# A hybrid encoder on one core: the first two weight jobs of a layer done by halves of the tokens

## The chip, the cores and the metric

The kernel runs on one core of one Trainium2 chip. The metric is the device time of one execution in microseconds; where several runs are given, their median.

## What is computed

Two layers, each with one mixer of two parallel groups, 256 tokens, model width 2048, all in float32. Cut to what matters here:

```python
x = layer_norm(x, ln_emb_g, ln_emb_b)
for l in range(DEPTH):                       # DEPTH = 2
    proj = einsum('bsd,de->bse', x, w_in[l])  # 2048 -> 6144
    u, g_ssm, q, k, v, g_attn = split(proj)
    y = u * ssm_d + s5_scan(u, forward) + s5_scan(u, reverse)
    y = gelu(y);  y = y * sigmoid(y @ w_glu[l] + b_glu[l]);  y_ssm = y * silu(g_ssm)
    lam = exp(sum(lambda_q1 * lambda_k1)) - exp(sum(lambda_q2 * lambda_k2)) + lambda_init
    o = diff_attention(rotary(q), rotary(k), v, lam)
    y_attn = rms_norm(o, attn_norm_g[l]) * (1 - lambda_init) * silu(g_attn)
    x = layer_norm(ALPHA * x + concat(y_ssm, y_attn) @ w_out[l], ln_g[l], ln_b[l])
return x
```

## The kernel before

Every large product is made of three float32r products: both operands are split into a high part, rounded to float32r, and a low part, the rest, and `mm3` (lines 167 to 170) adds high by high (line 168), high by low of the activations (line 169) and low of the weights by high (line 170).

The weights come in **jobs** of 512 by 256 values (`jobs`, line 124; 272 of them). `load` (line 143) fetches a job on SP's queue into one of four `raw` buffers; `do_split` (line 155) makes `wh` on ScalarE (line 162) and `wl` on VectorE (line 164), two jobs ahead of their use, in three buffers; `sub_step` (line 841) then issues 24 products of 128x128 weights by 256 tokens (2 column blocks, 4 contraction tiles, 3 products). The first eight jobs of a layer are the first two column blocks of the input projection, taken alternately for each quarter of the contraction, into two PSUM tiles `acc2`; every later block takes its four jobs one after the other.

The activations stand with the contraction on the partitions. They get there by the **layer norm** `ln_finish` (line 214), a generator that the program advances by `next(ln)`: moments on VectorE and GpSimd, `centre` (line 229) and `norm` (line 235) on VectorE, transposes on TensorE (line 248), and the split into `xh` (ScalarE, line 252) and `xl` (VectorE, line 253). It works on two sets of 128 rows (tokens), i = 0 and 1. Rows 0 come first for the first contraction tiles (four tiles before layer 0, eight before layer 1), then rows 1, then the rest of both. In the kernel before, the first product of a layer waits until rows 1 are there as well, since each takes all 256 tokens. Before layer 0 the input is loaded and normalised; before layer 1 the norm follows the last two output blocks of layer 0 (lines 987 to 1012), which are themselves done for rows 0 first, then for rows 1.

**Side work** runs between the jobs: `side` (line 778), called once a job, advances generators (`Lane`) for the SSM's tables (`ssm_tables`, line 295), operand loads and transposes (`ssm_load`, line 403; lines 421 and 446), the SSM's input, scan and output, the attention heads, and the stores of x for the residual. A generator's second yielded number is how many jobs it stays away.

The order in which instructions stand in each engine's queue is made by a scheduler that simulates the program's time; `after(ins)` (line 115) ties what is issued under it behind an instruction. SP's queue, like the others, is in order. Small loads stand in SP's queue among the weights: lambda's four vectors and the norm's gain `gsc` (`lam_of`, lines 661 and 673, called at the beginning of a layer), the tables' eight (lines 302 to 305), `ssm_d` (line 435), `b_glu` (line 955). `newest[0]` holds the latest weight load.

Of the kernel before, what the change touches and what calls it, by code (L numbers as in the profile page):

```python
# [8 lines left out]
F32 = mybir.dt.float32  # L9
F32R = mybir.dt.float32r  # L10
AF = mybir.ActivationFunctionType
# [9 lines left out]
KT = 4  # L21
# [11 lines left out]
RAW_BUFS = 4  # L33
SPLIT_AHEAD = 2
BUDGET = 1.6
# [2 lines left out]
LOAD_HOP = 10  # L38
SCAN_COST = 1.0
HEAD_HOPS = (1,1,2,2,2,3)  # L40


@with_exitstack
def kernel(
# [34 lines left out]
    def T(shape, tag, bufs=1, dt=F32):  # L79
        return sb.tile(shape, dt, tag=tag, name=tag, bufs=bufs)  # L80
# [33 lines left out]
    @contextmanager  # L114
    def after(ins):

        if ins is None:
            yield
        else:
            with tc.issue_after(ins):  # L120
                yield
# [16 lines left out]
        for cb in range(8):  # L138
            jobs += [(l, "out", cb, 0), (l, "out", cb, 1)]
    raws, split = {}, {}  # L140
    newest = [None]

    def load(i):
        if i >= len(jobs):
# [10 lines left out]
    def do_split(i, wh=None, wl=None, behind=None):  # L155
        if i >= len(jobs):
            return
        raw = raws.pop(i)
        if wh is None:
            wh = T([128, KT, 256], "wh", SPLIT_AHEAD + 1, F32R)  # L160
            wl = T([128, KT, 256], "wl", SPLIT_AHEAD + 1, F32R)
        A.copy(wh, raw)  # L162
        with after(behind):
            V.tensor_tensor(wl, raw, wh.bitcast(F32), sub)  # L164
        split[i] = (wh, wl)

    def mm3(o, lh, ll, rh, rl, first, last):
# [46 lines left out]
    def ln_finish(r, gt, bt, st, dst, box, ahead):  # L214


        pool = [None]

        def moments(i):
            mv = T([128, 2], "mv", 2)  # L220
            V.bn_aggr(mv, st[:, i].rearrange("p c s -> p (c s)"))
            rstd = T([128, 1], "rstd", 2)
            GP.tensor_scalar(rstd, mv[:, 1:2], EPS, None, add)
            pool[0] = GP.tensor_tensor(rstd, rstd, mhalf[:, 0:1], ALU.pow).ins
            return mv, rstd

        def centre(i, k0, nk, mv):
            cs = slice(k0 * 128, (k0 + nk) * 128)
            V.scalar_tensor_tensor(r[:, i, cs], r[:, i, cs], mv[:, 0:1], gt[:, cs], sub, mult)

        def norm(i, k0, nk, mv, rstd):
            cs = slice(k0 * 128, (k0 + nk) * 128)
            if dst is None or i == 0:
                centre(i, k0, nk, mv)
            last = V.scalar_tensor_tensor(r[:, i, cs], r[:, i, cs], rstd, bt[:, cs], mult, add)  # L235
            if dst is None:
                stores.append((xres[128 * i:128 * i + 128, cs], r[:, i, cs]))
            else:
                for j in range(2):
                    SY.dma_start(dst[2 * i + j][:, cs], r[64 * j:64 * j + 64, i, cs])  # L240
            return last.ins

        def trans(k0, nk, i0, ni):

            t = ss_bank([128, nk, 128 * ni])
            for k in range(nk):
                for i in range(ni):
                    PE.transpose(t[:, k, 128 * i:128 * i + 128],
                                 r[:, i0 + i, (k0 + k) * 128:(k0 + k + 1) * 128], ident)
            sl = (slice(None), slice(k0 % 8, k0 % 8 + nk), slice(128 * i0, 128 * (i0 + ni)))  # L250
            h, lo_ = box[0].h[k0 // 8][sl], box[0].l[k0 // 8][sl]
            A.copy(h, t)  # L252
            V.tensor_tensor(lo_, t, h.bitcast(F32), sub)  # L253

        mv, rstd = moments(0)
        if dst is None:
            box[0] = Pair()
        m0 = mv, rstd
        last = None
        for k0 in range(0, ahead, 4):  # L260
            nk = min(ahead - k0, 4)
            with after(last if k0 else None):
                last = norm(0, k0, nk, *m0)
            if dst is None:
                trans(k0, nk, 0, 1)
        yield
        mv, rstd = moments(1)
        if dst is None:
            box[0].more()
        if dst is not None:  # L270
            k0 = k1 = 0
            for nk in LAST_PIECES + (0,):
                if nk:
                    with after(last):
                        centre(1, k0, nk, mv)
                if k0:
                    last = norm(1, k1, k0 - k1, mv, rstd)
                k0, k1 = k0 + nk, k0
            return
        for k0, nk in ((0, 2), (2, 2), (4, 4), (8, 4), (12, 4)):  # L280
            for i, m in ((0, m0), (1, (mv, rstd)))[k0 < ahead:]:
                with after(last):
                    last = norm(i, k0, nk, *m)
            box[1] = last, pool[0]
            if dst is None:
                if k0 < ahead:
                    trans(k0, nk, 1, 1)
                else:
                    for k in range(k0, k0 + nk, 2):
                        trans(k, 2, 0, 2)  # L290
            if k0 != 0 or ahead < 8:
                yield


    def ssm_tables():
# [3 lines left out]
        ls = T([128, 2], "p_ls")  # L299
        for l in range(2):  # L300
            ps = slice(64 * l, 64 * l + 64)
            SY.dma_start(lr[ps].rearrange("g (d p) -> g d p", d=2), ssm_lam_re[l].rearrange("d g p -> g d p"))
            SY.dma_start(li[ps].rearrange("g (d p) -> g d p", d=2), ssm_lam_im[l].rearrange("d g p -> g d p"))
            for d in range(2):
                SY.dma_start(ls[ps, d:d + 1], ssm_log_step[l, d].unsqueeze(1))
        step = T([128, 2], "p_st")
        A.activation(step, ls, AF.Exp)
        for d in range(2):
            dsl = slice(64 * d, 64 * d + 64)
            V.tensor_scalar(zr[:, dsl], lr[:, dsl], step[:, d:d + 1], None, mult)  # L310
            V.tensor_scalar(zi[:, dsl], li[:, dsl], step[:, d:d + 1], None, mult)
        mag = t1
        A.activation(mag, zr, AF.Exp)
        yield 1.0, 1
# [88 lines left out]
    def ssm_load(l):  # L403
# [28 lines left out]
        z.dd = T([128, 16], "dd")  # L432
        GP.memset(z.dd, 0.0)
        for gi in range(4):
            SY.dma_start(
                z.dd[32 * gi:32 * gi + 16, :],
                ssm_d[l].rearrange("(q g c) -> g c q", g=4, c=16)[gi],
            )
        z.C = T([128, 2, 64, 16], "c8")
        Cv = z.C.rearrange("p r (o g) c -> p r o (g c)", o=8)  # L440
        yield 0.0, 1
# [213 lines left out]

    swap = list(range(8, 16)) + list(range(0, 8)) + list(range(16, 32))

    def lam_of(l):
        t = T([128, 4, 64], "on")
        for i, src in enumerate((lambda_q1, lambda_k1, lambda_q2, lambda_k2)):  # L660
            SY.dma_start(t[:, i, :], src[l:l + 1, :].to_broadcast([128, 64]))
# [10 lines left out]
        gs = T([128, 1], "gsc", 2)  # L672
        SY.dma_start(gs, attn_norm_g[l].unsqueeze(1))
        V.tensor_scalar(gs, gs, 1.0 - init, None, mult)
        return neg, gs

# [139 lines left out]
    box = {}  # L816
    ln = ln_finish(r, gt, bt, st, None, box, 4)
    for i in range(2):
        for c in range(8):
# [1 line left out]
        if i == 0:  # L821
            next(ln)
    for i in range(SPLIT_AHEAD):
        next(ln)
        do_split(i, behind=box[1][0])
        load(RAW_BUFS + i)
    ji = 0

# [9 lines left out]
    def acc_bank():  # L838
        return PS([128, 2, 256], "acc", 2)
# [19 lines left out]
    def block(hi, lo, n=4, tok_major=False):  # L859
        acc = acc_bank()  # L860
        for s in range(n):
            sub_step(acc, s, hi, lo, 0, n * KT - 1, tok_major)
        return acc

    for l in range(DEPTH):
        if l:
            next(ln)
        X = box[0]
        if l == 0:
            l_load = Lane(ssm_load(0), 1)  # L870
            l_tab = Lane(ssm_tables(), 1)
# [11 lines left out]
            z.ublocks = b + 1  # L883

        l_store = Lane(store_x(), 1.5)
        neg, gsc = lam_of(l)
        hi, lo = X.hi, X.lo
        acc2 = [acc_bank(), acc_bank()]
        for s in range(4):
            for b in range(2):  # L890
                sub_step(acc2[b], s, hi, lo, 0, 15, k_outer=True)
                if s == 3:
                    u_done(b, acc2[b])
                if b == 0 and s < 3:
                    next(ln)
            if s == 2:
                l_in = Lane(ssm_in(l), 3, after=[l_load, l_tab])
        l_in.after.append(l_store)
        for b in (2, 3):
            u_done(b, block(hi, lo))  # L900
        l_scan = Lane(ssm_scan(l), 5, after=[l_in])
        oT = T([128, 8, 256], "a8", 3)
        store = {}
# [48 lines left out]
        finish(l_out)  # L952
        V.tensor_tensor(z.yT, sgs, z.yT, mult)
        bg = T([128, 8], "bg", 2)
        SY.dma_start(bg, b_glu[l].rearrange("(o p) -> p o", p=128))
# [121 lines left out]
```

## Time and profile before

| | us |
|---|---|
| median of 3 runs | 1005.09 (1001.4 to 1006.62) |
| profiled execution, its own time | 1002.55 |
| span of that execution | 1000.8 |
| TensorE: products in flight | 955.8 |
| TensorE: weight loads | 926.8 |
| VectorE busy | 780.3 |
| ScalarE busy | 576.0 |

The profile shows one execution. PE is TensorE's products, PEld its weight loads, which overlap the products; DVE is VectorE, ACT ScalarE, POOL GpSimd, SP the queue that issues the DMAs here. A product's listed duration (about 0.28 us) is longer than the step from one product to the next, since products are pipelined; steps are read from the starts. A group of rows gives the line, the engine, the operation, the tile that it writes and the tiles that it reads; line numbers are those of the kernel before.

### The profile page before, as it was taken

The page shows a single profiled execution, that of the slowest core. Times are in us where ns is not written, and L with a number is a line of the kernel's source. Part 1 is how long each engine was busy: PE and PEld are TensorE (multiplying, and loading weights), DVE is VectorE, ACT ScalarE, POOL GpSimd, SP SyncE. Part 2 cuts the span into 40 slices and gives each one's busy share as a digit, 9 for nine tenths or more (in the row PEclk, how much of TensorE's full clock was granted, in tenths as well). Part 3 has the DMA queues.
Part 4 walks back from the last instruction along what each step waited for, and adds up shares of the span by engine and source line. Part 5 has one row for each costly group of instructions (what it writes and reads, how often), then busy time and mean ns, then how long its engine had stood idle before and what let it go on. Part 6 is the DMA issues. An engine that isn't in the chain of part 4 may idle for free.

```text
span 1000.8 us, 24625 instructions
## 1 busy us (share of the span) xinstructions
PE 955.8 (96%) x10304; PEld 926.8 (93%) x10304; DVE 780.3 (78%) x1353; ACT 576.0 (58%) x950; POOL 71.7 (7%) x103
## 2 busy tenths in 40 slices
PE   2999999999999998999979999999999999999995
PEld 2989988999999998999979989999999999999995
DVE  6875799899887786656588699899899759565676
ACT  2546588565575697545344585555556769843640
POOL 1000130210200000000011030010100100000001
PEclk9999999999999999999989999999999999999998
DMA  9898521545554643779875724555445454576953
GB/s 272 254 256 230 184 81 44 168 149 169 156 183 153 193 145 104 234 228 260 215 231 167 233 68 126 170 169 161 157 150 187 151 168 136 178 237 209 270 173 85
DMA packets 193167, 177.76 MB, mean 178 GB/s; under 512 B 37536, under 2 KB 185760, under 8 KB 193056
## 3 DMA queue, kind: packets, MB, share of 16 engines
q1 hardware_dynamic: 193056, 176.18, 58.7%
q8 instruction: 81, 1.33, 0.6%
q14 instruction: 30, 0.25, 0.1%
HBM read 165.02 MB, written 11.14 MB: 176 GB/s over the span
## 4 chain that ended last, share of the span: by engine, by line
PE 81%; DMA 7%; DVE 6%; ACT 3%; issue 1%; SPq 1%; POOL 0%; POOLq 0%; DVEq 0%; ACTq 0%
PE acc L168 23%; PE acc L169 23%; PE acc L170 23%; DMA raw<-in_w_out_dram 3%; PE ss L596 2%; DVE wl L164 2%; PE ss L501 1%; PE sc L707 1%; PE ss L735 1%; PE tp L473 1%; ACT wh L162 1%; PE tp L577 1%; DVE w L456 1%; DVE H L235 1%; DMA H<-in_x_dram 1%
## 5 line engine op out<-in xcount | busy, mean ns | idle before, releaser
L164 DVE TENSOR_TENSOR wl<-raw,wh 128x1024 fp32r<-128x1024 f32 x266 | 324.9, 1223 | 143.0 <-ACT wh L162 141.8
L162 ACT CAST wh<-raw 128x1024 fp32r<-128x1024 f32 x266 | 278.2, 1050 | 251.0 <-PE acc L169 118.7
L168 PE MATMUL acc<-xh,wh 128*128 128x256 f32 x1280 | 370.9, 290 | 0.8 <-ACT xh L252 0.5
L169 PE MATMUL acc<-xl,wh 128*128 128x256 f32 x1280 | 365.2, 286 | 0.8 <-DVE xl L253 0.7
L170 PE MATMUL acc<-xh,wl 128*128 128x256 f32 x1280 | 364.1, 285 | 1.1 <-DVE wl L164 1.1
L168 PEld LDWEIGHTS acc<-xh,wh 128*128 128x128 f32 x1280 | 245.5, 192 | 6.2 <-ACT xh L252 1.4
L169 PEld LDWEIGHTS acc<-xl,wh 128*128 128x128 f32 x1280 | 245.7, 192 | 2.4 <-DVE xl L253 1.5
L170 PEld LDWEIGHTS acc<-xh,wl 128*128 128x128 f32 x1280 | 245.6, 192 | 2.1 <-DVE wl L164 1.5
L168 PE MATMUL acc<-wh,xh 128*128 128x256 f32 x512 | 146.3, 286 | 0.0
L169 PE MATMUL acc<-wl,xh 128*128 128x256 f32 x512 | 145.4, 284 | 0.0
L170 PE MATMUL acc<-wh,xl 128*128 128x256 f32 x512 | 145.0, 283 | 0.0
L169 PEld LDWEIGHTS acc<-wl,xh 128*128 128x128 f32 x512 | 98.2, 192 | 0.2
L168 PEld LDWEIGHTS acc<-wh,xh 128*128 128x128 f32 x512 | 98.1, 192 | 0.1
L170 PEld LDWEIGHTS acc<-wh,xl 128*128 128x128 f32 x512 | 98.2, 192 | 0.0
L169 PE MATMUL acc<-wl,a 128*128 128x256 f32 x208 | 59.1, 286 | 2.1 <-DVE wl L164 2.1
L168 PE MATMUL acc<-wh,a 128*128 128x256 f32 x208 | 58.7, 284 | 0.0
L170 PE MATMUL acc<-wh,a 128*128 128x256 f32 x208 | 58.5, 283 | 0.0
L551 DVE TENSOR_TENSOR sa<-tab,H 128x256 f32<-128x256 f32 x126 | 53.0, 421 | 2.9 <-ACT H L504 0.7
L458 DVE TENSOR_TENSOR w<-w,x 128x512 f32<-128x512 f32 x64 | 45.6, 712 | 0.8
L169 PEld LDWEIGHTS acc<-wl,a 128*128 128x128 f32 x208 | 39.7, 191 | 3.3 <-DVE wl L164 3.3
L717 ACT ACTIVATE e<-sc,mx 128x256 f32<-128x256 f32 x64 | 29.5, 477 | 21.0 <-DVE mx L711 21.0
L168 PEld LDWEIGHTS acc<-wh,a 128*128 128x128 f32 x208 | 39.7, 191 | 0.4 <-ACT wh L162 0.4
(198 smaller groups left out, 1482.9 us busy)
## 6 DMA issues: line engine op xcount, KB each, us to landing
raw<-in_w_in_dram SPq DMA_DIRECT2D x192, 512.0 KB, 3.8
raw<-in_w_out_dram SPq DMA_DIRECT2D x64, 512.0 KB, 4.6
raw<-in_w_glu_dram SPq DMA_DIRECT2D x16, 512.0 KB, 4.4
xr<-xres SPq DMA_DIRECT2D x16, 256.0 KB, 4.3
xres<-H SPq DMA_DIRECT2D x14, 256.0 KB, 3.4
H<-in_x_dram SPq DMA_DIRECT2D x8, 256.0 KB, 5.9
u_dr<-ub SPq DMA_DIRECT2D x8, 256.0 KB, 3.3
a<-u_dr SPq DMA_DIRECT2D x8, 256.0 KB, 3.8
```

What stands on the lines that cost most here:

```text
L162: A.copy(wh, raw)
L164: V.tensor_tensor(wl, raw, wh.bitcast(F32), sub)
L168: PE.matmul(o, lhsT=lh, rhs=rh, start=first, stop=False, skip_group_check=True)
L169: PE.matmul(o, lhsT=lh, rhs=rl, start=False, stop=False, skip_group_check=True)
L170: PE.matmul(o, lhsT=ll, rhs=rh, start=False, stop=last, skip_group_check=True)
L235: last = V.scalar_tensor_tensor(r[:, i, cs], r[:, i, cs], rstd, bt[:, cs], mult, add)
L456: V.tensor_tensor(dst, t.unsqueeze(2).to_broadcast([128, 8, 16, 4]), M[:, m, gs, :].unsqueeze(3).to_broadcast([128, 8, 16, 4]), mult)
L458: V.tensor_tensor(w[:, r], w[:, r], x2, op)
L473: PE.transpose(t[:, pr, :], ws[o][:, ri, 2 * pr:2 * pr + 2].rearrange("p g c j -> p (g c j)"), ident)
L551: V.tensor_tensor(a.rearrange("p v q r g -> p v q (r g)"), lam, h.unsqueeze(1).to_broadcast([128, 2, 16, 8]), mult)
L596: PE.matmul(yps[d][halves[g2], pr, :], lhsT=w[halves[d], ri, g].rearrange("p c j -> p (c j)"), rhs=h[:, ::-1] if d else h, start=ri == 0, ...
L717: A.activation(e[:, m, i, :], sc[:, m, i, :], AF.Exp, bias=mx[:, c:c + 1], accum_out=sm[:, c:c + 1])
```

## The change

The first two jobs of each layer are issued by a new function, `by_halves`: first both jobs' products for the first 128 tokens, then each job's for the other 128. A job so has 48 products of 128 tokens instead of 24 of 256. In layer 0 the first halves are issued before the norm of rows 1, in layer 1 before the `next(ln)` that brings rows 1. The split of jobs 0 and 1 is no longer tied behind the norm of rows 1 (`behind=box[1][0]` is gone), that of job 2 is tied behind the split of the newest transposed activations. Lambda's loads move from the beginning of a layer to behind its eighth job and its arithmetic to behind the fourth block; the tables' arithmetic starts three jobs later; the small loads stand behind the newest weight load, and their first arithmetic behind the newest split.

```diff
+TAB_HOP = 3
...
-    newest = [None]
+    box = {}
+    newest = [None] * 4
...
-        A.copy(wh, raw)
-        with after(behind):
-            V.tensor_tensor(wl, raw, wh.bitcast(F32), sub)
+        first = box[2] if i == 2 else (box.get(3) if i < 2 else None, behind)
+        with after(first[0]):
+            newest[2] = A.copy(wh, raw).ins
+        with after(first[1]):
+            newest[1] = V.tensor_tensor(wl, raw, wh.bitcast(F32), sub).ins
...
-            A.copy(h, t)
-            V.tensor_tensor(lo_, t, h.bitcast(F32), sub)
+            box[2] = A.copy(h, t).ins, V.tensor_tensor(lo_, t, h.bitcast(F32), sub).ins
...
+            with after(newest[0]):
+                SY.dma_start(lr[ps].rearrange("g (d p) -> g d p", d=2), ssm_lam_re[l].rearrange("d g p -> g d p"))
...
+        yield 0.0, TAB_HOP
         step = T([128, 2], "p_st")
-        A.activation(step, ls, AF.Exp)
+        with after(newest[2]):
+            A.activation(step, ls, AF.Exp)
         for d in range(2):
+            with after(newest[1]):
+                V.tensor_scalar(zr[:, dsl], lr[:, dsl], step[:, d:d + 1], None, mult)
+                V.tensor_scalar(zi[:, dsl], li[:, dsl], step[:, d:d + 1], None, mult)
...
-    def lam_of(l):
+    def lam_load(l):
         t = T([128, 4, 64], "on")
+        gs = T([128, 1], "gsc", 2)
+        with after(newest[0]):
+            for i, src in enumerate((lambda_q1, lambda_k1, lambda_q2, lambda_k2)):
+                SY.dma_start(t[:, i, :], src[l:l + 1, :].to_broadcast([128, 64]))
+            SY.dma_start(gs, attn_norm_g[l].unsqueeze(1))
+        return t, gs
+
+    def lam_of(l, t, gs):
...
     for i in range(SPLIT_AHEAD):
-        next(ln)
-        do_split(i, behind=box[1][0])
+        do_split(i)
         load(RAW_BUFS + i)
...
+    def by_halves(accs, h, blocks=(0, 1)):
+        hs = slice(128 * h, 128 * h + 128)
+        for b in blocks:
+            wh, wl = split[ji + b]
+            for k in range(KT):
+                for m in range(2):
+                    ms = slice(m * 128, (m + 1) * 128)
+                    mm3(accs[b][:, m, hs], wh[:, k, ms], wl[:, k, ms], X.hi(k)[:, hs], X.lo(k)[:, hs],
+                        h == 0 and m == 0 and k == 0, False)
...
     for l in range(DEPTH):
+        X = box[0]
+        acc2 = [acc_bank(), acc_bank()]
         if l:
+            by_halves(acc2, 0)
             next(ln)
...
-        neg, gsc = lam_of(l)
-        acc2 = [acc_bank(), acc_bank()]
-        for s in range(4):
+        if l == 0:
+            by_halves(acc2, 0)
+            for _ in range(2):
+                next(ln)
+        by_halves(acc2, 1, (0,))
+        do_split(ji + SPLIT_AHEAD)
+        load(ji + SPLIT_AHEAD + RAW_BUFS)
+        side(BUDGET)
+        next(ln)
+        by_halves(acc2, 1, (1,))
+        do_split(ji + SPLIT_AHEAD + 1)
+        load(ji + SPLIT_AHEAD + RAW_BUFS + 1)
+        for _ in range(2):
+            split.pop(ji)
+            ji += 1
+        side(BUDGET)
+        for s in range(1, 4):
...
         for b in (2, 3):
+            if b == 2:
+                lam = lam_load(l)
             u_done(b, block(hi, lo))
+        with after(newest[1]):
+            neg, gsc = lam_of(l, *lam)
```

`ssm_d`'s and `b_glu`'s loads get the same `with after(newest[0])`.

## Rows read from the trace of the kernel before

**Rows 1.** The page: busy time of each engine, share of the span, instructions.
```profile
PE 955.8 (96%) x10304; PEld 926.8 (93%) x10304; DVE 780.3 (78%) x1353; ACT 576.0 (58%) x950; POOL 71.7 (7%) x103
```

**Rows 2.** TensorE's waits over the whole span: us in total, times, longest.
```profile
PE ss L248 <- DVE H L235: 18.9, 4, 12.0
PE tp L446 <- DMA a<-in_ssm_c_re_dram: 4.3, 1, 4.3
```

**Rows 3.** Stretches at the layer boundary: busy us (instructions), PEclk, DMA share, GB/s.
```profile
516.00:518.00 2.00, 0.71 (x6) 0.52 (x5) 2.00 (x6) 1.41 (x3) 0.00 (x0) 1.00 1.19 313
518.00:520.00 2.00, 0.00 (x0) 0.00 (x0) 1.53 (x5) 0.00 (x0) 1.20 (x2) 0.63 1.11 298
520.00:522.00 2.00, 0.98 (x5) 1.01 (x6) 1.93 (x5) 0.00 (x0) 0.00 (x0) 0.50 0.90 262
```

**Rows 4.** Timeline of the start: start us, us, engine, line, operation.
```profile
15.85 1.04 ACT L162 CAST wh<-raw 128x1024 fp32r<-128x1024 f32 x1 [2.14 <-DMA raw<-in_w_in_dram]
16.22 0.67 DVE L253 TENSOR_TENSOR xl<-ss,xh 128x512 fp32r<-128x512 f32 x1
18.86 1.22 DVE L164 TENSOR_TENSOR wl<-raw,wh 128x1024 fp32r<-128x1024 f32 x1
21.24 0.41 PE L170 MATMUL acc<-xh,wl 128*128 128x256 f32 x1
```

**Rows 5.** Timeline of TensorE: one product at the low clock, two in the stream.
```profile
23.16 0.41 PE L170 MATMUL acc<-xh,wl 128*128 128x256 f32 x1
...
125.79 0.28 PE L168 MATMUL acc<-xh,wh 128*128 128x256 f32 x1
127.47 0.28 PE L170 MATMUL acc<-xh,wl 128*128 128x256 f32 x1
```

**Rows 6.** Timeline around line 735; then groups by form: busy us, mean ns.
```profile
172.79 1.05 PE L735 MATMUL ss<-v,wT 128*128 128x128 f32 x8
173.60 0.36 PE L168 MATMUL acc<-xh,wh 128*128 128x256 f32 x1
...
L735 PE MATMUL ss<-v,wT 128*128 128x128 f32 x128 | 16.8, 274 | 0.0
L735 PEld LDWEIGHTS ss<-v,wT 128*128 128x128 f32 x128 | 15.6, 191 | 0.0
L577 PEld LDWEIGHTS tp<-cst,kw 128*64 128x64 f32 x256 | 8.9, 140 | 1.3
L482 PEld LDWEIGHTS tp<-w,cz 128*32 128x32 f32 x512 | 8.6, 109 | 3.3 <-issue 3.1
```

**Rows 7.** Timeline of TensorE in layer 0: where it waited for rows' parts.
```profile
26.17 0.55 PE L248 MATMUL ss<-cst,H 128*128 128x128 f32 x3 [0.53 <-DVE H L235]
27.17 0.39 PE L169 MATMUL acc<-xl,wh 128*128 128x256 f32 x1 [0.45 <-DVE xl L253]
44.33 0.39 PE L169 MATMUL acc<-xl,wh 128*128 128x256 f32 x1 [0.21 <-DVE xl L253]
```

**Rows 8.** Timeline of ScalarE and VectorE: waits for small loads.
```profile
36.04 0.20 ACT L307 ACTIVATE p_st<-p_ls 128x2 f32<-128x2 f32 x1 [2.80 <-DMA p_ls<-in_ssm_log_step_dram]
43.52 0.15 DVE L674 TENSOR_SCALAR gsc<-gsc 128x1 f32<-128x1 f32 x1 [2.49 <-DMA gsc<-in_attn_norm_g_dram]
```

**Rows 9.** Timeline of VectorE and TensorE at the layer boundary.
```profile
516.47 0.68 DVE L253 TENSOR_TENSOR xl<-ss,xh 128x512 fp32r<-128x512 f32 x1
520.67 0.48 DVE L235 SCALAR_TENSOR_TENSOR H<-H,rstd 128x256 f32<-128x256 f32 x1
521.02 1.94 PE L446 MATMUL tp<-cst,a 128*128 128x128 f32 x8 [4.31 <-DMA a<-in_ssm_c_re_dram]
530.84 0.28 PE L168 MATMUL acc<-xh,wh 128*128 128x256 f32 x1
```

**Rows 10.** Instructions of tile bh: duration ns min/median/max, first and last start.
```profile
L168 PE MATMUL acc<-bh,wh x55: 279/279/282, 440.7 to 459.8; 128*128 128x256 f32 x55
L630 DVE TENSOR_TENSOR c<-a,bh x4: 681/684/693, 396.9 to 411.8; 128x512 fp32r<-128x512 f32 x4
```

More of the change, by code (lines that the diff above doesn't have):

```diff
@@ L301, in ssm_tables @@
             ps = slice(64 * l, 64 * l + 64)
[L302 to L305, printed above, removed]
+            with after(newest[0]):
+                SY.dma_start(lr[ps].rearrange("g (d p) -> g d p", d=2), ssm_lam_re[l].rearrange("d g p -> g d p"))
+                SY.dma_start(li[ps].rearrange("g (d p) -> g d p", d=2), ssm_lam_im[l].rearrange("d g p -> g d p"))
+                for d in range(2):
+                    SY.dma_start(ls[ps, d:d + 1], ssm_log_step[l, d].unsqueeze(1))
+        yield 0.0, TAB_HOP
         step = T([128, 2], "p_st")
-        A.activation(step, ls, AF.Exp)
+        with after(newest[2]):
+            A.activation(step, ls, AF.Exp)
         for d in range(2):
             dsl = slice(64 * d, 64 * d + 64)
-            V.tensor_scalar(zr[:, dsl], lr[:, dsl], step[:, d:d + 1], None, mult)
-            V.tensor_scalar(zi[:, dsl], li[:, dsl], step[:, d:d + 1], None, mult)
+            with after(newest[1]):
+                V.tensor_scalar(zr[:, dsl], lr[:, dsl], step[:, d:d + 1], None, mult)
+                V.tensor_scalar(zi[:, dsl], li[:, dsl], step[:, d:d + 1], None, mult)
         mag = t1
@@ L434, in ssm_load @@
         for gi in range(4):
[L435 to L438, printed above, removed]
+            with after(newest[0]):
+                SY.dma_start(
+                    z.dd[32 * gi:32 * gi + 16, :],
+                    ssm_d[l].rearrange("(q g c) -> g c q", g=4, c=16)[gi],
+                )
         z.C = T([128, 2, 64, 16], "c8")
@@ L656 @@
     swap = list(range(8, 16)) + list(range(0, 8)) + list(range(16, 32))
-    def lam_of(l):
+    def lam_load(l):
         t = T([128, 4, 64], "on")
-        for i, src in enumerate((lambda_q1, lambda_k1, lambda_q2, lambda_k2)):
-            SY.dma_start(t[:, i, :], src[l:l + 1, :].to_broadcast([128, 64]))
+        gs = T([128, 1], "gsc", 2)
+        with after(newest[0]):
+            for i, src in enumerate((lambda_q1, lambda_k1, lambda_q2, lambda_k2)):
[3 more added lines that the diff above has]
+    def lam_of(l, t, gs):
         tv = t.rearrange("p (m k) d -> p m k d", m=2)
@@ L671, in lam_of @@
         V.scalar_tensor_tensor(neg, e2[:, 1:2], -init, e2[:, 0:1], add, sub)
-        gs = T([128, 1], "gsc", 2)
-        SY.dma_start(gs, attn_norm_g[l].unsqueeze(1))
         V.tensor_scalar(gs, gs, 1.0 - init, None, mult)
@@ L815 @@
     st = T([128, 2, 8, 6], "st")
-    box = {}
     ln = ln_finish(r, gt, bt, st, None, box, 4)
@@ L863, in block @@
         return acc
+    def by_halves(accs, h, blocks=(0, 1)):
[7 more added lines that the diff above has]
+                        h == 0 and m == 0 and k == 0, False)
     for l in range(DEPTH):
+        X = box[0]
+        acc2 = [acc_bank(), acc_bank()]
         if l:
+            by_halves(acc2, 0)
             next(ln)
-        X = box[0]
         if l == 0:
@@ L954 @@
         bg = T([128, 8], "bg", 2)
-        SY.dma_start(bg, b_glu[l].rearrange("(o p) -> p o", p=128))
+        with after(newest[0]):
+            SY.dma_start(bg, b_glu[l].rearrange("(o p) -> p o", p=128))
         M.h.append(T([128, 8, 256], "a8", 3, F32R))
```

## The prediction, made before the change was timed

> **What bounds the kernel now.** I read the page first: TensorE has a product in flight for 955.8 of 1000.8 us and its weight loads fill 926.8 us [rows 1]. So a microsecond is worth something only where TensorE stands still or takes up more work. The list of TensorE's waits names two places of size [rows 2]: 18.9 us in four waits of the layer norm's transposes, 12.0 of it the wait at the very start, and 4.3 us for the DMA of an SSM operand. The chain of waits agrees (its main part is the products of lines 168 to 170), and the stretches of 2 us around the layer boundary show the second hole: TensorE does next to nothing from 516 to 520 us, and its granted clock falls to 0.63 and 0.50, the lower of its two levels [rows 3]. At the start, the first product that reads a low part wl issues at 21.24 us [rows 4]. The change fills both holes with products of the first 128 tokens and pays with narrower products. What a narrow product costs decides, so it comes first.
>
> **Price of a narrow product.** In the stream a 256-column product takes a step of 0.120 us: 14 steps from 125.79 to 127.47 [rows 5]. At the low clock, 9 steps from 21.24 to 23.16 make 0.213 each [rows 4, 5]. The change turns the first two jobs of each layer, 48 such products, into 96 with 128 columns, each with a weight load of its own of the same 128x128 size. No float32r product of 128 columns is in the trace. The nearest row is line 735: 128x128 weights, 128 columns, plain float32, eight in a run from 172.79, the last ending at 173.84: (1.05 - 0.274) / 7 = 0.111 us a step [rows 6]. Half the columns saved 7%, not 50%. The reason stands in the weight loads: 109 ns at 32 weight columns, 140 at 64, 191 at 128 [rows 6], a slope of (191 - 109) / 96 = 0.85 ns a column, so 109 ns of loading for 128 columns, and the load is not halved here. I take 0.111. Lower bound: half a step, 0.060, if the loads hide. Upper bound: two passes of 0.111, as line 735 itself needs (128 records for 64 products in the source).
> The Trainium skill speaks otherwise: "TensorE: Matmul & The Clock Gate", section "Back-to-back issue gap", gives about 81 ns a product for a sustained stream of weight loads and products of 128 columns. By it the sum below would be 192 x 0.030 = 5.8 us lower, an estimate; line 735 speaks against it here.
>
> **Layer 0, step by step.** (a) Start: wh of job 0 is ready at 15.85 + 1.04 = 16.89, and xl of rows 0 at 16.22 + 0.67 = 16.89. The subtraction for wl waits behind the norm of the other rows until 18.86 and takes 1.22. The change takes that tie off, so it can run from 16.89 to 18.11, and the stream starts at 18.1, not 21.24 [rows 4]: -3.1. (b) Work: 96 x 0.111 - 48 x 0.120 = 10.66 - 5.76 = +4.9. At the low clock some 14 products pass in either kernel, so about nothing more (+0.1). (c) TensorE's waits of 0.53 and 0.45 us for rows 1 [rows 7] lie under the first half's products, which last until 18.1 + 14 x 0.213 + 34 x 0.111 = 24.9: -1.0. What remains late there is VectorE's chain for rows 1 (norm, copy, difference), to which wl of jobs 0 and 1 are now put in front, 2.4 us; it ended at about 27.1 before [rows 7] and has to be there by 25 to 26, which it can, since those two subtractions stood within it before. (d) Two transposes of rows 1 that ran ahead of the stream now cut it: 2 x 0.11 + a break of 0.08 (0.36 against 0.28 for the product after a break [rows 6]) = +0.3. (e) The small loads. VectorE stood 2.49 us before gsc and ScalarE 2.80 us before p_st, both for DMAs, in queues that also make xl and wh [rows 8]; TensorE felt it as waits like that of 44.33 [rows 7]. Lambda and tables now come behind the newest split or load: -0.5 (0 to -1.0).
> Sum of layer 0: -3.1 + 4.9 + 0.1 - 1.0 + 0.3 - 0.5 = +0.7.
>
> **Layer 1.** The first xl of rows 0 is ready at 516.47 + 0.68 = 517.15, and 48 full products then end at 530.84 + 0.12 = 530.96 [rows 9]: 13.8 us. After: 96 x 0.111 = 10.7 from 517.15, without the low clock since TensorE no longer idles; the transposes that stood in the hole (4 of rows 1, the 8 of line 446 [rows 9]) and 4 more are now in the stream, 16 x 0.111 = 1.8, with four breaks, 0.3. That is 12.8. Rows 1 are normalised at 520.67 + 0.48 = 521.15 [rows 9]; with transpose, copy and difference (about 1.5 us, an estimate from 0.37 to 0.42 a piece for two pieces) they are ready at 522.7, when the first half has ended (517.15 + 5.33 = 522.5): +0.2. Layer 1: 12.8 + 0.2 - 13.8 = -0.8.
>
> **What is moved at no cost.** Per layer the five DMAs of lambda and gsc, with the tables' eight and ssm_d's four, move on SP's queue behind a weight load. Each holds SP for about half a microsecond; the loads gain where they stood behind them, and in layer 1 five issues (2 us) lie among loads that run four buffers, some 11 us, ahead. If that cover failed TensorE would wait those 2 us. The tables come three jobs (9 us) later; the SSM's result is split by 411.8 + 0.7 and first read at 440.7 [rows 10], so 28 us cover it. The waits placed by hand put splits ahead of small operations; behind a small operation stands only its own chain.
>
> **How the numbers follow.** +0.7 - 0.8 = -0.1 us: the two covers are paid back almost exactly by the weight loads that are done twice. The profiled execution took 1002.55 us (span 1000.8), 2.5 under the median of 1005.09, so I forecast 1005.0 us, with a range of its own from 1001 to 1009, for the order in which the scheduler mixes 100-odd transposes into the stream will differ (a break is 0.1 to 0.2 us). I count 0.5% (5 us) as the least that a measurement can tell from no change.
>
> **Rivals.**
> 1. Narrow products are cheap (0.060 to 0.081 us). For it: the columns alone would need half a step. Against: line 735 and the slope of the weight loads. Then rows 1 set the second halves: layer 1 ends at 522.7 + 48 x 0.060 + 8 transposes 0.9 = 526.5, -4.4; layer 0 can gain some -2.3 until VectorE's chain binds. Together -6.7: 998.4 us. Chance 0.25, the pace named by the skill (999.2) being 0.10 of it.
> 2. Slower: a narrow float32r product runs as two passes, like the float32 one in rows 6. Price 192 x 0.111 = +21 less the cover that grows with it (some 2): 1024 us. It decides from a step of 0.111 + 5 / 192 = 0.137 us upward. For it: the trace has no float32r product under 256 columns. Against: nothing shows float32r splitting. Chance 0.07.
> 3. TensorE's queue is in order, and the wait of 4.31 us for ssm_c [rows 9] is put ahead of the halves. Then they start at 521.02 + 0.9 and end near 535, with the low clock again: +4 to layer 1, 1009.5. For it: it is just what the order was before. Against: the halves stand earlier in the program. Chance 0.13, half of it beyond +0.5%.
> 4. The change doesn't do what it says: the scheduler leaves the halves behind the other rows in layer 1, so the weight loads are paid without cover: +0.7 + 4.9, 1010.7. Chance 0.05.
> The forecast keeps 0.50 (0.03 faster, 0.42 same, 0.05 slower). Faster: 0.03 + 0.22 = 0.25. Slower: 0.05 + 0.07 + 0.06 + 0.05 = 0.23. Same: 0.52. The range, 998 to 1010.5, leaves out half of rival 1's low end, rival 2 and part of rival 4.
>
> **What would show it.** Right: a step of about 0.11 between narrow products; the first wl product near 18 us; TensorE busy from 517 to 531 with the clock at 1.0, yet its first two jobs ending within 1 us of 530.96; layer 0's about 0.7 us later than before. Wrong: steps of 0.06 or 0.2, line 446 waiting ahead of the halves, or rows 1 later than the first half's end.

## The result and the profile after

The changed kernel takes 1012.85 us (median of four runs, 1012.53 to 1014.2) beside 1003.95 us for the kernel before: a ratio of 1.0108, 95% interval 1.0086 to 1.013. It is slower by 8.9 us, above the range that was given (998 to 1010.5). The profiled execution after took 1014.2 us (span 1012.3).

The page of after, busy time of each engine, shows where to look first. Beside [rows 1] the span grew by 11.5 us, TensorE's products by 11.9 and its weight loads by 16.3; VectorE has 2.0 us more, ScalarE 3.1 less. TensorE has more to do, or does it more slowly.

```profile
PE 967.7 (96%) x10400; PEld 943.1 (93%) x10400; DVE 782.3 (77%) x1353; ACT 572.9 (57%) x948; POOL 71.4 (7%) x103
```

TensorE's waits in after (us in total, times, longest) show two things beside [rows 2]: the transposes' waits fell from 18.9 to 12.1 and the 4.3 us for ssm_c are gone, as the change meant; but of the former 4.0 us stand now as a wait for wh ahead of the first narrow product, and a wait of 5.0 us for ssm_b_im has come that the kernel before did not have.

```profile
PE ss L252 <- DVE H L239: 12.1, 2, 11.7
PE acc L172 <- ACT wh L166: 5.1, 2, 4.0
PE tp L428 <- DMA a<-in_ssm_b_im_dram: 5.0, 1, 5.0
```

To place the loss in time I read, in TensorE's timelines of both kernels, when the same share of the main products has been issued (a narrow product counts one half):

| full products issued | before, us | after, us | after later by |
|---|---|---|---|
| 1 | 20.15 | 17.07 | -3.1 |
| 24 | 25.01 | 29.03 | +4.0 |
| 48 (end of the first two jobs) | 30.22 | 39.36 | +9.1 |
| 336 | 71.99 | 76.7 | +4.7 |
| 384 | 79.3 | 91.18 | +11.9 |
| 3264 (last of layer 0) | 514.1 | 523.83 | +9.7 |
| 3312 (end of layer 1's first two jobs) | 530.72 | 539.64 | +8.9 |
| 6528 (last of all) | 988.58 | 1000.22 | +11.6 |

So the first two jobs of layer 0 lose 9.1 us. Up to product 336 after wins 4.4 back, then loses 7.2 by product 384, of which 5.0 are the wait for ssm_b_im. Layer 1's boundary gains 0.8. Behind it after loses another 2.7 in these two executions, which lie 11.7 us apart where the medians lie 8.9; where that comes from is not shown. The other places are read one by one.

**The first jobs of layer 0.** The timeline of the start of after: the start came forward as planned, for wl is made at 17.42 and the first product with it issues at 18.69, not 21.24 [rows 4].

```profile
16.03 0.67 DVE L256 TENSOR_TENSOR xl<-ss,xh 128x512 fp32r<-128x512 f32 x1
16.80 0.47 PE L172 MATMUL acc<-xh,wh 128*128 128x128 f32 x1 [4.01 <-ACT wh L166]
17.42 1.22 DVE L168 TENSOR_TENSOR wl<-raw,wh 128x1024 fp32r<-128x1024 f32 x1
18.69 0.48 PE L174 MATMUL acc<-xh,wl 128*128 128x128 f32 x1 [1.20 <-DVE wl L168]
```

TensorE's timeline further on, 14 to 20 us later, shows the pace:

```profile
32.02 0.41 PE L173 MATMUL acc<-xl,wh 128*128 128x128 f32 x1
32.23 0.41 PE L174 MATMUL acc<-xh,wl 128*128 128x128 f32 x1
34.37 1.93 PE L252 MATMUL ss<-cst,H 128*128 128x128 f32 x8
35.95 0.46 PE L172 MATMUL acc<-xh,wh 128*128 128x128 f32 x1
37.48 0.37 PE L173 MATMUL acc<-xl,wh 128*128 128x128 f32 x1
37.69 0.28 PE L174 MATMUL acc<-xh,wl 128*128 128x128 f32 x1
37.80 0.27 PE L172 MATMUL acc<-xh,wh 128*128 128x128 f32 x1
```

A narrow product steps by 0.213 us (32.02 to 32.23) up to 37.69 us and by 0.111 from there on. That is the low clock: 0.213 is also the step of a full product at the start of the kernel before [rows 4, 5], 0.111 the one forecast for the high clock. The PEclk column prints 1.00 over this whole stretch, since the trace's records of the granted clock only begin at 37.66 us, with the full clock (in the kernel before at 23.61); ahead of the first record it is the steps that tell the level. In the kernel before, the high clock was there at 23.6 us, 3.5 us after the first full product. Here TensorE worked without a gap from 18.69 us, and 80 of the 96 narrow products (the first two ahead of that gap) still passed at the low one.

**Layer 1.** In stretches of 2 us there (busy us of each engine with counts, PEclk, DMA share, GB/s), the hole of [rows 3] is gone: TensorE is busy at least 1.59 of 2 us, at the high clock. The narrow products near 539 us step by 0.11.

```profile
522.00:524.00 2.00, 2.00 (x19) 2.00 (x18) 2.00 (x4) 0.00 (x0) 0.00 (x0) 1.00 0.34 131
524.00:526.00 2.00, 1.59 (x13) 1.33 (x12) 2.00 (x4) 1.89 (x4) 0.00 (x0) 1.00 0.60 168
526.00:528.00 2.00, 1.73 (x15) 1.54 (x14) 2.00 (x6) 1.15 (x3) 0.00 (x0) 1.00 1.20 306
```
```profile
538.97 0.28 PE L174 MATMUL acc<-xh,wl 128*128 128x128 f32 x1
539.08 0.28 PE L172 MATMUL acc<-xh,wh 128*128 128x128 f32 x1
539.19 0.27 PE L173 MATMUL acc<-xl,wh 128*128 128x128 f32 x1
```

**The new wait.** TensorE's timeline and SP's queue in after: lambda's loads (lines 671 and 672) take SP from 60.35 to 64.3, a few others among them, ssm_b's two loads (line 420) follow at 69.42 and 71.54, and the transposes that need the second stand still until 81.99.

```profile
81.99 1.09 PE L428 MATMUL tp<-cst,a 128*128 128x128 f32 x4 [5.01 <-DMA a<-in_ssm_b_im_dram]
```
```profile
60.35 0.50 SPq L671 DMA_DIRECT2D on<-in_lambda_q_dram  x1
...
63.91 0.43 SPq L672 DMA_DIRECT2D gsc<-in_attn_norm_g_dram  x1
...
69.42 2.08 SPq L420 DMA_DIRECT2D a<-in_ssm_b_re_dram  x1
71.54 0.62 SPq L420 DMA_DIRECT2D a<-in_ssm_b_im_dram  x1
```

In the kernel before those two loads issued at 55.40 and 57.62, and the first of their transposes, at 80.63, waited for nothing.

The wait has a second cost. The stretch right behind it (columns as for layer 1) has the low clock, PEclk 0.50; the kernel before has no such stretch between 23.6 and 388 us. Full products step by 0.21 there (two steps from 84.64 to 85.07). The 16 products and transposes in it, each some 0.1 us slower, make 1.6 us, an estimate, of the 2.2 that the wait leaves of the 7.2.

```profile
82.00:85.40 3.40, 3.40 (x16) 3.06 (x17) 1.36 (x2) 2.26 (x4) 0.00 (x0) 0.50 0.94 333
```

**The tables' transposes.** What after wins back between is a gain that was not forecast. TensorE's timelines, of the kernel before, then of after:

```profile
60.32 0.27 PE L374 MATMUL tp<-cst,a 64*128 64x64 f32 x1
60.96 0.27 PE L374 MATMUL tp<-cst,a 64*128 64x64 f32 x1
```
```profile
88.43 0.46 PE L381 MATMUL tp<-cst,a 64*128 64x64 f32 x4
```

Between 56 and 79 us the kernel before has 16 of these transposes, 12 alone and 4 in two pairs. One alone cuts the stream of products: around that of 60.32 the steps are 0.21, 0.20 and 0.22 us where two products take 0.24, so 0.39 for one. In after, where the tables come three jobs later, they stand in fours, and a four costs 0.58 (in a timeline of an experiment below, e12, 0.82 from 77.56 to 78.38 less 0.24). Twelve single ones and two pairs at 0.45 make 5.6 us, four fours 2.3: 3.3 us less work in the stream, an estimate.

### The profile page after: what moved, and what is told of

It reads as the page before. It is cut to its first block, busy times and chain, and to the rows that moved or that the text cites. A ratio compares the mean times of both kernels' runs of the same rounds, so it can differ in the third digit from the quotient of the medians.

```text
span 1012.3 us, 24822 instructions
## 1 busy us (share of the span) xinstructions
PE 967.7 (96%) x10400; PEld 943.1 (93%) x10400; DVE 782.3 (77%) x1353; ACT 572.9 (57%) x948; POOL 71.4 (7%) x103
## 4 chain that ended last, share of the span: by engine, by line
PE 86%; DVE 4%; ACT 4%; DMA 2%; issue 1%; SPq 1%; POOL 0%; POOLq 0%; DVEq 0%; ACTq 0%
PE acc L172 25%; PE acc L173 24%; PE acc L174 24%; PE ss L604 2%; PE ss L509 2%; PE ss L747 1%; PE sc L719 1%; PE tp L481 1%; DMA a<-in_ssm_b_im_dram 1%; ACT wh L166 1%; DVE wl L168 1%; DMA H<-in_x_dram 1%; DVE H L239 1%; ACT H L512 1%; PE tp L585 1%
## 5 line engine op out<-in xcount | busy, mean ns | idle before, releaser
L172 PE MATMUL acc<-xh,wh 128*128 128x256 f32 (+1 forms) x1312 | 382.2, 292 | 4.2 <-ACT wh L166 4.0
L174 PE MATMUL acc<-xh,wl 128*128 128x256 f32 (+1 forms) x1312 | 375.7, 287 | 2.0 <-DVE wl L168 2.0
L173 PE MATMUL acc<-xl,wh 128*128 128x256 f32 (+1 forms) x1312 | 375.9, 287 | 0.7 <-DVE xl L256 0.7
L172 PEld LDWEIGHTS acc<-xh,wh 128*128 128x128 f32 x1312 | 254.8, 194 | 8.8 <-ACT wh L166 4.4
L174 PEld LDWEIGHTS acc<-xh,wl 128*128 128x128 f32 x1312 | 255.1, 194 | 3.0 <-DVE wl L168 2.4
L173 PEld LDWEIGHTS acc<-xl,wh 128*128 128x128 f32 x1312 | 255.3, 195 | 1.5 <-DVE xl L256 0.9
```

The lines of the kernel that those rows point to most:

```text
L172: PE.matmul(o, lhsT=lh, rhs=rh, start=first, stop=False, skip_group_check=True)
L173: PE.matmul(o, lhsT=lh, rhs=rl, start=False, stop=False, skip_group_check=True)
L174: PE.matmul(o, lhsT=ll, rhs=rh, start=False, stop=last, skip_group_check=True)
```

## The experiments

The theory after this reading: (A) layer 0's halves lose because a narrow stream runs at the low clock; (B) lambda's new place in SP's queue makes the wait for ssm_b_im. Rivals: the narrow products or the new order are dear in themselves, whatever the clock; the wait comes from the order that the halves make in TensorE's queue.

**Parts of the change alone.** `e1_narrow_l1_moves` is the change with layer 0's first jobs at full width; `e2_narrow_l1` is the kernel before with halves in layer 1 only; `e3_narrow_both` has halves in both layers and the small loads where they were; `e4_moves` has the moves and no halves. The core of e1's edit, which in e2 stands on the loop of the kernel before (e3 leaves the condition out, e4 leaves all of it out):

```diff
-        by_halves(acc2, 1, (0,))
-        ...
-        for s in range(1, 4):
+        if l == 1:
+            by_halves(acc2, 1, (0,))
+            ...
+        for s in range(int(l == 1), 4):
```

> The whole change, but layer 0's first two jobs are issued at full width (256 tokens) as before. In the changed kernel the first two jobs of layer 0 end 9.0 us later than before, all 80 narrow products up to 37.6 us stepping at 0.213 us; near 77 us TensorE waits 5.0 us for the DMA of ssm_b_im. Theory A (the low clock stays on because narrow products stand at the start of layer 0): layer 0's first two jobs end near 30 us again, the total falls by some 8 to 9 us, to about 1004 to 1007 depending on whether the wait near 77 us stays. Theory B (the moved small loads delay layer 0): it stays within 2 us of 1012.9.

> Before, with halves in layer 1 alone and nothing else of the change. Theory A: in the changed kernel the boundary ended 0.9 us earlier against the time of its last product of layer 0, so 1 us faster than before, 1003 us, with a narrow step of 0.111 us and the clock staying up from 517 to 531 us. Rival (a narrow product is always slow, or the wait for ssm_c stands ahead of the halves): 4 us or more slower than before.

> Halves in both layers, but lambda, the tables and the other small loads placed as before. Theory A: the 9 us of the start stay, the 5.0 us wait for ssm_b_im near 77 us goes, because that load no longer stands behind lambda's five in SP's queue: about 3 us less than the whole change, 1009 to 1010 us. Theory B (the small loads' places make the start slow): layer 0's first two jobs end near 31 to 32 us and the total is about 1004 to 1005.

> Before, with the moved small loads, tables and lambda alone, no halves. Theory A: the start as before; the wait for ssm_b_im appears and costs up to 4 us: 1005 to 1008. Theory B: the start is late by 5 us or more, 1010 or above. A third possibility: the moves are neutral because the wait needs the late start as well, 1003 to 1005.

| kernel | us | before, same chip | ratio, 95% |
|---|---|---|---|
| e1: change, layer 0 at full width | 1006.24 | 1002.87 | 1.0033 (1.002 to 1.0045) |
| e2: halves in layer 1 only | 1002.58 | 1002.87 | 1.0003 (0.9986 to 1.002) |
| e3: halves in both layers, no moves | 1009.21 | 1002.87 | 1.0078 (1.0051 to 1.0105) |
| e4: moves alone | 1005.96 | 1002.87 | 1.003 (1.0009 to 1.0051) |

The parts add: halves in layer 0 cost 7.5 us (e3 less e2: 0.75%; the change less e1: 0.75%), the moves 3 us (e4; e1 less e2), halves in layer 1 nothing that the time can tell. In e2's profile the boundary gains 0.8 us, in e1's too, as in after: from the last product of layer 0 to the last of layer 1's first two jobs it takes 15.8 us in all three, 16.6 in the kernel before. But e4, at full width, takes 14.7 (513.17 to 527.87), and so does e7 below; there the wait for ssm_c is 2.8 us instead of 4.3 [rows 9] and the low clock lasts 2.9 and 3.5 us from the end of that wait on, instead of 4.3. Beside these, the halves in layer 1 lose 1.1 us. One profile of each does not tell whether the moves shortened that wait or the executions differ.

```profile
519.50 1.85 PE L454 MATMUL tp<-cst,a 128*128 128x128 f32 x8 [2.83 <-DMA a<-in_ssm_c_re_dram]
```

In e3 all 96 narrow products pass at the low clock; TensorE's timeline shows the last of them and what came next:

```profile
41.22 0.41 PE L173 MATMUL acc<-xl,wh 128*128 128x128 f32 x1
41.43 0.41 PE L174 MATMUL acc<-xh,wl 128*128 128x128 f32 x1
41.64 0.73 PE L172 MATMUL acc<-xh,wh 128*128 128x256 f32 x2
...
45.38 0.34 PE L172 MATMUL acc<-xh,wh 128*128 128x256 f32 x1
45.55 0.28 PE L173 MATMUL acc<-xl,wh 128*128 128x256 f32 x1
45.67 0.28 PE L174 MATMUL acc<-xh,wl 128*128 128x256 f32 x1
```

The narrow stream ran 22 us, from 19.23 to 41.64, and the clock did not rise; it rose at 45.5, 3.8 us into the full products. No wait for ssm_b_im stands in e3; in e4, which has no halves at all, TensorE waits 6.2 us for it. So that wait belongs to the moves, not to the halves' order.

**Lambda's place.** `e7_moves_not_lambda` is e4 with lambda's loads and arithmetic back at the beginning of the layer; `e9_l1_moves_not_lambda` does the same to e1.

```diff
+        neg, gsc = lam_of(l, *lam_load(l))
...
-            if b == 2:
-                lam = lam_load(l)
...
-        with after(newest[1]):
-            neg, gsc = lam_of(l, *lam)
```

> The moved loads without the halves (as in the run of the moves alone), but lambda's five loads and its arithmetic at the beginning of the layer as before. In the run of the moves alone TensorE waits 6.2 us near 67 to 74 us for ssm_b_im, which SP issued at 62.8 us, behind lambda's five loads, while the transposes that need it stand some 70 products earlier in TensorE's queue than before. If lambda's place in SP's queue makes the wait: it shrinks by the 3 to 5 us that the five loads took, and the total returns to 1002.5 to 1004. If the transposes' earlier place makes it (they are early because the tables' arithmetic is late): the wait stays above 3 us and the total at 1005 to 1006.

> The parts of the change that cost nothing by themselves, together: halves in layer 1 alone, and the moved loads without lambda (0.998 of before by themselves). If the parts add up: 0.997 to 0.999 of before, 999 to 1001 us, with no wait for ssm_b_im. If halves in layer 1 or the moves bring that wait back: 1003 or more.

e7 took 999.64 us beside 1001.92 (0.9982, 0.9958 to 1.0005), 4.8 us better against its reference than e4. e9 took 998.85 beside 1003.01 (0.9966, 0.9947 to 0.9986), 6.7 us better than e1 and faster than the kernel before. SP's queue and TensorE's timeline, first of e4, then of e7:

```profile
52.84 0.92 SPq L671 DMA_DIRECT2D on<-in_lambda_q_dram  x1
...
60.57 2.19 SPq L420 DMA_DIRECT2D a<-in_ssm_b_re_dram  x1
62.81 0.62 SPq L420 DMA_DIRECT2D a<-in_ssm_b_im_dram  x1
...
73.82 1.09 PE L428 MATMUL tp<-cst,a 128*128 128x128 f32 x4 [6.23 <-DMA a<-in_ssm_b_im_dram]
```
```profile
55.04 0.63 SPq L420 DMA_DIRECT2D a<-in_ssm_b_re_dram  x1
...
57.23 1.02 SPq L420 DMA_DIRECT2D a<-in_ssm_b_im_dram  x1
...
69.48 0.62 PE L428 MATMUL tp<-cst,a 128*128 128x128 f32 x4
```

Without lambda's loads ahead of them ssm_b's two issue 5.5 us sooner, and the transposes wait for nothing. The transposes also stand earlier in TensorE's queue with the moves (69.48 in e7, 80.63 in the kernel before, at nearly the same pace of products). In e4 the load arrives at 73.82, ahead of the 80.63 at which the kernel before wanted it, so by these times the new wait takes both (no run moves lambda alone). (B) holds: taking lambda's place back is enough. The low clock at that place, up to 4.0 us behind the wait in e4 and 3.6 in e1, is gone with it in e7 and e9. The other moves gain: 1.8 us in e7 by the medians of the runs (0.18%, with an interval that just includes nothing) and 3.7 between e9 and e2 (0.37%), near the 3.3 of the tables' transposes, which stand in fours in e7 and e9 too. No run delays the tables alone, so that they are the cause is argued, not shown. e9 and e7 can't be told apart (their intervals overlap): halves in layer 1 are not shown to gain here either.

**The clock.** `e5_warm` is the whole change with 70 and 60 products ahead of the first narrow one; they have 256 columns, read constants and write a PSUM tile that nobody reads. `e10_warm_short` has 24 in place of the 60.

```diff
+    warm(70, wr[:, 0])
...
+            box[9] = warm(60, box[0].h[0][:, 0, 0:128])
```

> The whole change, with 130 products of 256 columns on constants issued ahead of layer 0's first product: 70 before the transposes of rows 0 and 60 behind them, into a PSUM tile that is not read until the heads overwrite it. They keep TensorE busy from about 2 to 20 us, so the clock is up when the narrow products begin; VectorE makes xl of rows 0 somewhat later, so these begin near 20.5 instead of 18.7 us. Theory A (the narrow products cost 0.213 us only because the clock is low, and cannot bring it up, but do not lose it): narrow steps of 0.111 from the first on, the first two jobs end near 33 us instead of 39.4, the total falls by 5 to 7 us to 1006 to 1008. Rival (narrow products drop the clock, or something else than the clock paces them in layer 0): steps return to 0.213 within some us and the total stays at 1012 to 1014.

> The whole change with the products on constants of the run before, 24 instead of 60 behind the transposes. There the second batch began at 17.2 us, behind ScalarE's xh, needed 3.6 us at the low clock to bring the clock up, and held the stream back until 26.0 us; from there on the narrow products stepped at 0.111 us. Now it should end near 21.6 us. Theory A (the low clock alone made the halves dear in layer 0): narrow steps of 0.111 from 21.6 on, the first two jobs end near 34 us instead of 39.4, the total falls by some 5 us, to 1007 to 1009. Rival (the narrow stream loses the clock when it is barely up, or waits for VectorE's parts of rows 1 take the gain): the first two jobs end after 37 us and the total stays within 2 us of 1012.9.

e5 took 1014.64 us (1.0133, 1.0094 to 1.0172), e10 1014.15 (1.0109, 1.0081 to 1.0137): both missed the totals expected of them. In e5 TensorE had to wait 3.7 us for ScalarE's xh between the two batches, the granted clock was 0.50 from 17.3 to 20.7 us, in the second batch, and the narrow stream began only at 25.95. But its 96 products then stepped at 0.111 and took 12.65 us with their transposes, beside 22.7 us in after. In e10 the first two jobs ended at 35.2 us, 4.1 before after's, and the total did not follow: the wait for ssm_b_im is now 5.9 us and the low clock lasts 5.1 us behind it, not 3.4. Of the 4.1 us, 2.5 are left at product 384, 1.2 at product 1000 and 0.2 at the last. Whether (A) governs the total was so still open, because (B)'s wait lay on top. Two more kernels without that wait settle it: `e12_halves_moves_not_lambda`, the whole change with lambda where it was (e7's edit), and `e13_warm_not_lambda`, e10 with the same edit.

> The whole change, with lambda's five loads and their arithmetic put back to the beginning of the layer. If lambda's place in SP's queue made the wait of TensorE for ssm_b_im, that wait (5.0 us in the changed kernel) is gone here, the first two jobs of layer 0 still end near 39 us at the low clock, and the time is that of the halves of layer 1 with the moves less lambda (0.9966 of the kernel before) and the 7.5 us that the halves of layer 0 cost: ratio 1.004, about 1007 us against 1003. Rival: the wait comes from the order that the halves of layer 0 make in TensorE's queue; then it stays and the ratio is 1.009 or more.

> As the run before it, with 70 and 24 products on constants (256 columns, their sums not used) ahead of the first narrow product, so that the clock is up when the halves of layer 0 begin. Theory (the cost of the halves in layer 0 is the low clock): the narrow products step at 0.111 us from about 22.7 us, the first two jobs end near 35 instead of 39, and the whole is 4 us shorter than the run before it, about 1003 us, ratio 1.000. Rival (what the narrow products lose at the start is made up or lost later by the order of the work, whatever the clock): the first two jobs end 4 us sooner, but the whole time is that of the run before it, within 1 us.

e12 took 1008.91 us (1.0059, 1.0034 to 1.0083), e13 1003.66 (1.0019, 1.0003 to 1.0035), beside 1002.36. TensorE's timeline in e12, then in e13:

```profile
41.40 0.41 PE L174 MATMUL acc<-xh,wl 128*128 128x128 f32 x1
41.62 0.73 PE L172 MATMUL acc<-xh,wh 128*128 128x256 f32 x2
...
46.42 0.34 PE L172 MATMUL acc<-xh,wh 128*128 128x256 f32 x1
46.60 0.27 PE L173 MATMUL acc<-xl,wh 128*128 128x256 f32 x1
```
```profile
17.68 5.49 PE L822 MATMUL sc<-wT,xh 128*128 128x256 f32 x24 [4.57 <-ACT xh L257]
22.97 0.31 PE L172 MATMUL acc<-xh,wh 128*128 128x128 f32 x1
...
25.92 0.28 PE L174 MATMUL acc<-xh,wl 128*128 128x128 f32 x1
26.04 0.28 PE L172 MATMUL acc<-xh,wh 128*128 128x128 f32 x1
...
35.72 0.33 PE L172 MATMUL acc<-xh,wh 128*128 128x256 f32 x1
```

The same 96 products of the same tiles end at 41.6 us at the low clock and at 35.7 at the high one, though the latter start 5.7 us later. The whole is 5.2 us shorter by the medians, 0.4% by the ratios (their intervals only just meet); in the two profiles TensorE stands 5.9 us apart at the end of the first jobs and 6.8 at the end of the program. (e12's profile is of the longest of its seven runs, 1012.8 us; two took 1003.25 and 1004.92, and whether its clock rose as late in every run is not shown.) So the early microseconds do carry through. Against e9, which differs from both only in layer 0, the halves cost 9.3 us at the low clock and 5.3 with 70 and 24 products spent to raise it. Of these 5.3, 4.9 stand at the end of the first jobs: e13's stream begins 2.3 us later than e9's full products (22.97 and 20.65) and takes 2.6 longer. So e13 does not show what the halves would cost with the clock up from the start at no price.

**Another way to fill the same holes.** `e6_v_first` and `e8_v_first` start from the kernel before and put the first quarter of two value blocks (16 and 17) at the head of each layer. In those blocks the tokens are the weights of the product and 256 weight columns stream, so a product takes only 128 tokens anyway: half the tokens can go first with no load done twice and no narrow product. e6 does the rest of these blocks right behind; e8 keeps the partial sums aside and does the rest at the blocks' old place. `e11_v_first_moves` is e8 with e7's moves. From e8's edit:

```diff
+        jobs += [(l, "in", 16, 0), (l, "in", 17, 0)]
...
+                mm3(accv[:, b, h, :], X.hi(k)[:, hs], X.lo(k)[:, hs], wh[:, k, :], wl[:, k, :],
+                    h == 0 and k == 0, k == KT - 1)
...
+                V.tensor_tensor(v, v, acc, add)
```

> Before, with the idea of the change kept and its price taken away: each layer begins with the first quarter of two value blocks (columns 16 and 17), whose products have the tokens as weights, so that a half of the tokens is half of the products, all with 256 columns; the other three quarters follow after the u blocks. No weight load is done twice: 24 products of 0.120 us are added to each hole and taken away later. Theory A (the holes can be filled, the doubled weight loads and the low clock ate it): layer 0 begins near 18 us with the clock rising as before, some 2 us gained; layer 1 gains 2.9 us plus the low clock, 3 to 4; total 4 to 6 us faster than before, 997 to 999. Rival (the hole is only moved: rows 1 end the wait whatever stands in it, or the queue order gets worse): within 2 us of before.

> The value blocks' first quarters ahead of each layer, as in the run of that name before, but their partial sums are copied out at once and the other quarters stay where the blocks were, so that the order of the later blocks and heads is that of before. There layer 0's first 48 products ended 1.8 us earlier than before and the layer boundary 4.3 us earlier, and the rest of the program lost 18 us in many waits for wl, wh and the SSM. Theory A (those losses came from the new order of the blocks, not from filling the holes): both gains stay, the total is 3 to 6 us below before, 996 to 999. Rival (two jobs more ahead of the u blocks make everything behind them late): no gain, 1001 to 1006.

> The value blocks' first quarters ahead of each layer, with their partial sums copied out, and the moved loads without lambda. If the two add up: 1 to 2 us below the run without the moves, 995 to 998 us. If a new order of the queues costs as much as the holes give: 1000 to 1006.

e6 took 1015.62 us (1.015, 1.0117 to 1.0183), far from the 997 to 999 expected: it gained 1.8 us at the start and 4.3 at the boundary, and the other order of the blocks cost some 19 in the rest of the program, with 10.1 us of waits for wl (3.2 in the kernel before) and smaller ones for wh and for side work. e8 took 997.39 beside 1003.01 (0.9939, 0.9918 to 0.996), faster than both kernels: the first two jobs end 2.2 us sooner and the boundary gains 4.2, with some 4 us given back elsewhere. e11 took 997.28 (0.9942, 0.9916 to 0.9968): the moves add nothing to it. TensorE's timeline of e8 at the boundary, where the full products of the first 128 tokens step by 0.12:

```profile
516.12 0.36 PE L169 MATMUL sc<-wh,xh 128*128 128x256 f32 x1
...
518.26 0.28 PE L169 MATMUL sc<-wh,xh 128*128 128x256 f32 x1
518.38 0.28 PE L170 MATMUL sc<-wl,xh 128*128 128x256 f32 x1
```

## Why the prediction was wrong

**The step that failed is (b) of layer 0, the term "+0.1" for the low clock.** It let "some 14 products" pass at the low clock "in either kernel", that is, it took the count from one profile of the kernel before as given, whatever stream ran. Measured: 80 narrow products in after, all 96 in e3 and e12. Even with full products the count is not fixed: 13 in e4, 24 in e7 and e9. In after 78 stepped at 0.213 from 18.69 on, 64 more than the 14 of the term; each 0.102 us slower, they make 6.5 us. Twelve transposes among them, also at the low clock, make some 1.0 more, an estimate (eight took 1.58 us, 34.37 to 35.95, beside 0.11 each at the high clock), and the stream with wl began 0.6 us later than forecast. Together 8.1, beside the 7.9 us by which the end of the first two jobs missed: +9.1 against +1.2 (the +0.7 without the small loads' -0.5, which lies later). e13 against e12 shows that the step is the clock's and not the products': with the clock up, the same products step at 0.111.

A step near 0.2 had been named as a sign that the forecast was wrong, and as rival 2, two passes. It was the other meaning of that number: at two passes the step would have stayed so in layer 1, where it is 0.111.

**The second failed step is "What is moved at no cost".** It priced lambda's five issues as 2 us among weight loads that run ahead. What it left out of the list of those queued behind them was ssm_b, whose loads do not run ahead, and that the delayed tables would let ssm_b's transposes come forward in TensorE's queue. Lambda's place cost 4.9 us (the change less e12), 4.8 (e4 less e7) and 6.7 (e1 less e9), where nothing, or 2 us, was forecast; in it are a wait of 5.0 to 7.1 us and, in the change, e1 and e4, 3.4 to 4.0 us at the low clock behind it. Rival 3 had this mechanism, a wait for an SSM operand at the head of TensorE's in-order queue, but in layer 1 and for ssm_c.

**What held.** The pace of 0.111 at the high clock, from line 735 and the slope of the weight loads, was measured in layer 1 and in e13. The Trainium skill ("TensorE: Matmul & The Clock Gate", section "Back-to-back issue gap") has about 81 ns for such a stream; these runs do not agree. The start moved to 18.69 us (18.1 forecast; first product 3.1 us sooner). Rows 1 did not make the halves wait. Layer 1 gained 0.8 us against the kernel before, as forecast; against e4 and e7, which have the moves and no halves, the same boundary lost 1.1. The moves, lambda's among them, were forecast at -0.5 us; without lambda's they gained 1.8 to 3.7, most likely in a way that the forecast did not see, the transposes in fours.

## What to carry to other kernels

Before splitting a product to start earlier, read at which clock the stretch runs, and do not assume that it will rise under the finer stream as it did under the coarse one: here layer 0's halves cost 9.3 us at the low clock and 5.3 with the clock raised first, and only an order in which the products stayed 256 columns wide (e8) gained at both ends. Of a small load that is moved, list every load queued behind it by the instruction that waits for it, and not only the stream that runs buffers ahead. A gain of some microseconds can be hidden by a second fault of the same size, so take the faults away one at a time, as e12 and e13 do, before a theory is given up.

## What the runs showed of the hardware

In every kernel without the products on constants, TensorE's clock was at the lower of its two levels when the first products began, by their steps of 0.213 us. Where these were full products of 256 columns, it rose 3.3 to 8.0 us after the first of them (before: 20.15 and 23.6; e4: 3.3 us; e7 and e9: 6.2; e8: 8.0, with a gap of 1.2 in it). A stream of 128-column products, one weight load each, ran 22 us in e3 and in e12 without a gap, and the lower level stayed; it rose 3.8 and 4.9 us into the full products behind it (e3: 41.64 and 45.5; e12: 41.62 and 46.5). The same stream begun at the higher level kept it: 12.65 us in e5, 12.75 in e13, and layer 1 of after. In after the clock did come up inside the narrow stream, at 37.7 us, some 1.7 us behind eight transposes; e3 and e12 had the same eight and it stayed down. What made that difference is open.

The Trainium skill ("TensorE: Matmul & The Clock Gate", section "What's actually happening") says that the throttled state is the default and that activity releases it. The traces agree that the low level comes first; in e3 and e12, where TensorE worked for 22 us without a gap and the level stayed, they do not agree that activity released it.

A wait of TensorE can cost more than its length: behind the waits for ssm_b_im of 5.0 to 7.1 us the granted clock was still 0.50 for 3.4 us in after, 3.6 in e1, 4.0 in e4, 5.1 in e10 and 6.4 in e5.
